# Layer 0's late modulation blocks moved from TensorE strips to running sums on VectorE, under a scheduler with three new rules

## The chip, the cores and the metric

The kernel runs on one core of a Trainium2 chip. The time of a kernel is the device time of one execution in microseconds (us), and what is given is the median of several executions. TensorE (PE in the rows) multiplies, VectorE (DVE) and ScalarE (ACT) do the elementwise work, SyncE (SP) and GpSimd (POOL) issue the transfers between HBM and the core's memory.

## The reference

A trunk of two layers over 256 context tokens and 256 latent tokens, D = 1024, float32. What matters here of each layer `i`:

```python
mod_l = jnp.split(sc @ ada_w[i] + ada_b[i], 6, axis=-1)          # sc = silu(c), one row
mod_c = jnp.split(sc_ctx @ ada_w[i] + ada_b[i], 6, axis=-1)      # the same for the context
y_l, y_c = hybrid_mixer(modulate(x, mod_l[0], mod_l[1]), modulate(ctx, mod_c[0], mod_c[1]), ...)
x = layer_norm(ALPHA * x + mod_l[2][:, None] * y_l, ln1_g[i], ln1_b[i])
x = layer_norm(ALPHA * x + mod_l[5][:, None] * swiglu(modulate(x, mod_l[3], mod_l[4]), ...), ...)
```

So the modulation is a product of two rows of length 1024 with a 1024 x 6144 matrix. Its blocks of 512 columns are numbered 0 to 11; blocks 0 to 3 are needed at the very start of a layer, blocks 4 to 11 only when the mixer's output projection ends and in the feed-forward part (FFN). The mixer has a Mamba-2 branch (convolutions, states by chunk), grouped-query attention and differential attention, merged by gates.

## The kernel before

**Work on the engines.** Every dense product is made in three fp32r passes: a weight tile is loaded raw, ScalarE copies its high part to a fp32r tile and VectorE subtracts that from the raw tile to get the low part (`load_w`, L756). So nearly each 512 KB of weights needs one ACT `CAST` and one DVE `TENSOR_TENSOR` `w<-w,w` before TensorE can use it. All other elementwise work of the branches (convolution taps in `conv`, L1149, softmax, rope, decay masks, chunk states in `chunk_state`, L1194) is on VectorE and ScalarE too.

**Order.** Nothing is issued as the code runs. Each operation is recorded in a `Plan`, with the buffers it touches; `schedule` (L312) then runs a list scheduler over modelled costs, in stretches of WINDOW modelled ns, tries TRIES = 8 sets of priorities for each stretch and keeps the best, and `emit` writes the instructions in that order. Each engine then runs its own list strictly in order on the chip and waits where an operand is not there. `pick` (L579) chooses an engine's next operation by priority, if its buffers fit (`allowed`, L503); `begin` (L649) books how long it takes and when it lands. Priorities follow the place of an operation in the recorded order, counted in TensorE time.

**Modulation.** There are two ways to make a block. `ada_parts` (L884) loads eight 128 x 512 tiles of the matrix and multiplies each on TensorE, four tiles side by side in strips of 32 columns of the array (`MATMUL ps<-s,s 128*32 128x512` in the rows, 8 records for a group of four, as an fp32 product is two). `ada_sums` (L922) loads the same tiles, and VectorE multiplies each by a column of `cond` (name `tiny`) and adds it to a running sum (`acc`, name `s`): for a sum one `TENSOR_SCALAR s<-s,tiny 128x512` and seven `SCALAR_TENSOR_TENSOR s<-s,tiny,s 128x512`; a group of four sums ends in one group of strips against `ones` (name `cst`) and four transposes. Before, layer 0 takes `ada_parts` for all twelve blocks and layer 1 takes `ada_sums`. Both use the same buffers of tag `aw`, eight at most.

**Where the late blocks stand in the recorded order.** In layer 0 the generator `ada_steps` is advanced beside the mixer, by the TensorE time that was spent:

```python
owed = advance(rest, owed + RATIO[i] * (spent() - s0))
owed2 = advance(adas, owed2 + 0.06 * (spent() - s0))
```

`advance` runs a generator until the TensorE time of what it recorded covers the cost that it was given.

Of the kernel before, what the change touches and what calls it, by code (L numbers as in the profile page):

```python
# [37 lines left out]
HOP, SLACK, SPARE = 300, 10000, 1  # L38
ENTER, LEAVE = 130, 90
GAP, REACH, BUMP = 200, 20000, 1.0  # L40
TRIES, WINDOW, AHEAD, WEIGHT = 8, 60000, 60000, 0.03

CAP = {"raw": 6, "aw": 8, "aw0": 32, "wh": 6, "wl": 6, "d": 6, "ada": 2, "row": 6, "yr": 3, "xa": 3, "re": 4}
RATIO = (1.52, 1.42)
# [373 lines left out]
class _State:  # L418
# [4 lines left out]
    def __init__(self, plan):  # L423
# [38 lines left out]
        self.cols, self.strip, self.order, self.mark, self.work = {}, False, [], 0, 0.0  # L462
        self.prio = None

    def copy(self):
        s = _State.__new__(_State)
        for k, v in self.__dict__.items():
            if k in ("plan", "room", "fifo", "prio"):
                pass
            elif k in ("load", "queue", "idle"):  # L470
                v = {c: x.copy() for c, x in v.items()}
            elif isinstance(v, (list, dict, np.ndarray)):
                v = v.copy()
            s.__dict__[k] = v
        s.mark = len(s.order)
        return s
# [23 lines left out]
                        break  # L500
        return best

    def allowed(self, b):  # L503
        c = b.cls
        if self.used[c] + b.units > self.room[c]:
            return False
        if b.cap and self.count[c, b.tag] >= b.cap:
            return False
        spot = None
        if c == "s2":  # L510
            spot = self.place(b)
            if spot is None:
                return False
        cur = self.cur
        if b.first > cur:
            seg = self.load[c][cur:b.first]
            if seg.max() + b.units > self.room[c]:
                return False
            if c == "s2":
                whole, part = b.units == 4, b.units if b.units < 4 else 0  # L520
                broken = sum(self.part_use) + (part > 0 and spot[0] == 4)
                small = self.small[cur:b.first]
                need = np.maximum((small + part + 3) // 4 + SPARE, broken)
                if ((seg - small) // 4 + whole + need).max() > self.plan.sizes["s2"]:
                    return False
        return True
# [52 lines left out]
    def pick(self, e):  # L579

        ops, sizes, q = self.plan.ops, self.plan.sizes, self.queue[e]
        skipped, pick, full = [], None, set()
        while q:
            item = heapq.heappop(q)
            new = [b for b in ops[item[1]].bufs if not self.held[b.seq] and b.cls in sizes]
            later = next((b for b in new if b.cap and self.fifo[b.cls, b.tag][self.head[b.cls, b.tag]] is not b), None)
            if later is not None:
                self.parked[later.seq] = self.parked.get(later.seq, ()) + (item[1],)
                continue
            if not new or (all(self.allowed(b) for b in new) and (len(new) < 2 or self.fits(new))):  # L590
                pick = item[1]
                break
            skipped.append(item)
            if len(skipped) > (24 if e == "SP" else 200):
                break
        for item in skipped:
            heapq.heappush(q, item)
        if pick is not None:
            for b in new:
                self.take(b)  # L600
        return pick

    def run(self, until):
        plan, ops = self.plan, self.plan.ops
        sizes, prio = plan.sizes, self.prio
        wait, running, frees, free = self.wait, self.running, self.frees, self.free
        heapq.heapify(wait)
        n = len(ops)
        while self.left and self.t < until:
            t = self.t  # L610
            while wait and wait[0][0] <= t:
                k = heapq.heappop(wait)[1]
                heapq.heappush(self.queue[ops[k].eng], (prio[k], k))
            while running and running[0][0] <= t:
                k = heapq.heappop(running)[1]
                self.done[k] = True
                self.left -= 1
                for b in ops[k].bufs:
                    self.bleft[b.seq] -= 1
                    if self.bleft[b.seq] == 0 and b.cls in sizes:  # L620
                        heapq.heappush(frees, (t + FREE, b.seq))
            while frees and frees[0][0] <= t:
                self.drop(plan.bufs[heapq.heappop(frees)[1]])
            while self.cur < n and self.done[self.cur]:
                self.cur += 1
            for e in self.ENGINES:
                if free[e] > t or not self.queue[e]:
                    continue
                pick = self.pick(e)
                if pick is not None:  # L630
                    self.begin(pick, e)
            nxt = []
            if wait:
                nxt.append(wait[0][0])
            if running:
                nxt.append(running[0][0])
            if frees:
                nxt.append(frees[0][0])
            nxt += [free[e] for e in self.ENGINES if free[e] > t and self.queue[e]]
            later = [x for x in nxt if x > t]  # L640
            if self.left and not later:
                if any(x <= t for x in nxt):
                    continue
                raise RuntimeError(f"no op can run at {t} ({self.left} left)")
            if later:
                self.t = min(later)
        return self

    def begin(self, k, e):  # L649
        ops, t = self.plan.ops, self.t  # L650
        op = ops[k]
        self.start[k] = t
        if op.nbytes:
            self.free[e] = t + op.dur
            self.dma_free = max(t + 1900, self.dma_free) + op.nbytes / 360.0
            end = self.dma_free + 950
        else:
            d = op.dur
            if e == "PE":
                c = int(t // TICK)  # L660
                cold = self.cols.get(c - 1, 0) < 3060
                if self.strip != op.strip:
                    d += ENTER if op.strip else LEAVE
                self.strip = op.strip
                self.cols[c] = self.cols.get(c, 0) + op.cols
                if cold:
                    d *= 2
                self.work += op.dur
            elif e != "SP":
                self.work += WEIGHT * op.dur  # L670
            end = t + d
            self.free[e] = end
        self.end[k] = end
        self.order.append(k)
        heapq.heappush(self.running, (end, k))
        for j in op.succs:
            e2 = ops[j].eng
            if op.nbytes:
                lat = 0
            elif e == e2:  # L680
                lat = 0 if e == "PE" else 127
            elif e == "PE":
                lat = 197
            elif e2 == "PE":
                lat = TO_PE
            else:
                lat = 145
            if end + lat > self.ready[j]:
                self.ready[j] = end + lat
            self.need[j] -= 1  # L690
            if self.need[j] == 0:
                heapq.heappush(self.wait, (self.ready[j], j))
# [20 lines left out]
def trunk(tc, x, c, cx, c_ctx, ada_w, ada_b, w_in, b_gate, conv_w, conv_b, dt_bias, a_log, ssm_d, norm_w,  # L713
# [5 lines left out]
    def t2(n=512, dt=F32, tag=None, cap=None):  # L719
        return plan.tile("s2", [128, n], dt, tag, cap)  # L720
# [4 lines left out]
    def th(n=128, tag=None, cap=None):  # L725
        return plan.tile("s2", [128, n], F32, tag, cap)
# [100 lines left out]
        V.tensor_copy(abias[i], ps[:, 0:48])  # L827

    def load_params(i):
        rows = [th(), th(), th()]  # L830
        r2 = lambda a: a.rearrange("(k p) -> k p", p=128)
        for o, n, src in ((C_BG, 24, r2(b_gate[i])), (C_CB, 24, r2(conv_b[i])),
                          (C_NW, 16, r2(norm_w[i])), (C_G1, 8, r2(ln1_g[i])), (C_B1, 8, r2(ln1_b[i]))):
# [13 lines left out]
        ps = psum()  # L847
# [220 lines left out]
    for (m, t0), xr in xraw.items():  # L1068
        xa = t2()
# [5 lines left out]
    for i in range(DEPTH):  # L1075
# [370 lines left out]

        def ada_steps():
            if i == 0:
                for ccs in ((4, 5, 6, 7), (8, 9, 10, 11)):
                    yield from ada_parts(0, ccs)  # L1450

        acc_d, t_d = dram([KT, 128, TN]), dram([KT, 128, TN])

# [74 lines left out]
        for d in range(KT):  # L1528
            w = load_w(w_ssm_out[i][D:2 * D, d * 128:(d + 1) * 128], KT, 128)
            ps = psd()  # L1530
            dense(ps[:, 0:TN], w, KT, lambda k: y[k])
            t, o = reload(t_d, d), reload(acc_d, d)
# [98 lines left out]
        for t0, r in segs:  # L1631
            for d in range(KT):
                xa = load_xa(xa_d, d, t0)
# [20 lines left out]
        for j0, j1 in ((0, 8), (8, 16), (16, 22)):  # L1654
# [26 lines left out]
            if j1 == 22 and not need_ctx:  # L1681
                xT_out = {(t, q): psum() for q in range(2) for t in range(2)}
                rows = {}
                for m, src in enumerate((ln2_g, ln2_b)):
                    for q in range(2):
                        rows[m, q] = t2()
                        G.dma_start(out=rows[m, q], in_=src[i][q * 512:q * 512 + 512].unsqueeze(0).to_broadcast([128, 512]))
            if need_ctx and j1 == 22:
                mc2 = mod_cols(i + 1, 0, (C_G2, C_B2, P))
# [110 lines left out]
```

## Time and profile before

| | us |
|---|---|
| median of 3 runs (2319.02 to 2319.55) | 2319.29 |
| profiled execution, its own time | 2322.81 |
| its span, first to last instruction | 2321.0 |
| TensorE busy in the span | 2263.6 |
| VectorE busy in the span | 1767.2 |
| ScalarE busy in the span | 1419.2 |

The profiled execution is 1.8 us longer than its span and 3.5 us above the median. The stages by the clock of the trace: start up to about 62 us, layer 0's mixer to about 1040, its FFN to about 1430, layer 1's mixer to about 2000, its FFN to the end. A busy time counts an instruction until its result is written; the next one of VectorE begins some 0.08 us before that, so the busy time of a full VectorE is its whole stretch, and work is counted best from start to start.

### The profile page before, as it was taken

The page shows a single profiled execution, that of the slowest core. Times are in us where ns is not written, and L with a number is a line of the kernel's source. Part 1 is how long each engine was busy: PE and PEld are TensorE (multiplying, and loading weights), DVE is VectorE, ACT ScalarE, POOL GpSimd, SP SyncE. Part 2 cuts the span into 40 slices and gives each one's busy share as a digit, 9 for nine tenths or more (in the row PEclk, how much of TensorE's full clock was granted, in tenths as well). Part 3 has the DMA queues.
Part 4 walks back from the last instruction along what each step waited for, and adds up shares of the span by engine and source line. Part 5 has one row for each costly group of instructions (what it writes and reads, how often), then busy time and mean ns, then how long its engine had stood idle before and what let it go on. Part 6 is the DMA issues. An engine that isn't in the chain of part 4 may idle for free.

```text
span 2321.0 us, 37955 instructions
## 1 busy us (share of the span) xinstructions
PE 2263.6 (98%) x13757; PEld 1914.9 (83%) x13757; DVE 1767.2 (76%) x3625; ACT 1419.2 (61%) x2873; POOL 138.7 (6%) x218
## 2 busy tenths in 40 slices
PE   8999999999999989999999999999999999999998
PEld 4876777777777778889888889888987779998997
DVE  3878856789988868799744338898789799868565
ACT  4767745677877564336424245787677687656553
POOL 3101101000100100000000000001010010000000
PEclk9999999999999999999999999999999999999999
DMA  9936454422533468896643324535643355786662
GB/s 322 290 90 192 147 142 142 110 78 83 157 96 91 141 177 268 282 312 179 215 121 100 99 76 130 148 112 171 182 130 100 97 137 158 202 266 192 195 183 88
DMA packets 516956, 371.48 MB, mean 160 GB/s; under 512 B 20739, under 2 KB 464515, under 8 KB 516769
## 3 DMA queue, kind: packets, MB, share of 16 engines
q1 hardware_dynamic: 503360, 329.63, 48.0%
q0 software_dynamic: 13408, 39.43, 5.9%
q8 instruction: 108, 1.77, 0.3%
q14 instruction: 80, 0.65, 0.1%
HBM read 335.17 MB, written 33.82 MB: 159 GB/s over the span
## 4 chain that ended last, share of the span: by engine, by line
PE 49%; DVE 6%; ACT 4%; DMA 4%; issue 2%; SPq 0%; ACTq 0%; POOL 0%; DVEq 0%; POOLq 0%
PE ps L415 49%; DVE s L415 3%; ACT s L415 2%; ACT shared L415 2%; DVE shared L415 2%; DMA s<-dram 1%; DMA shared<-dram 1%; DVE w L415 1%; DMA s<-in_ada_w_dram 1%; ACT w L415 1%; DVE tiny L415 0%; DMA w<-in_w_in_dram 0%; DMA w<-in_w_o_dram 0%; SPq L415 0%; POOL s L415 0%
## 5 line engine op out<-in xcount | busy, mean ns | idle before, releaser
L415 PE MATMUL ps<-s,w 128*128 128x512 f32 (+1 forms) x7560 | 1537.6, 355 | 3.2 <-DVE s L415 2.1
L415 PEld LDWEIGHTS ps<-s,w 128*128 128x128 f32 x7560 | 1238.7, 189 | 218.1 <-issue 30.0
L415 ACT CAST w<-w 128x1024 fp32r<-128x1024 f32 (+3 forms) x488 | 454.6, 940 | 399.8 <-DVE w L415 221.0
L415 DVE TENSOR_TENSOR w<-w,w 128x1024 fp32r<-128x1024 f32 (+3 forms) x488 | 528.4, 1087 | 194.6 <-PE ps L415 105.7
L415 PE MATMUL ps<-shared,w 128*128 128x256 f32 x2544 | 337.6, 285 | 5.4 <-ACT shared L415 5.3
L415 PEld LDWEIGHTS ps<-shared,w 128*128 128x128 f32 x2544 | 323.1, 193 | 8.6 <-ACT shared L415 6.6
L415 ACT ACTIVATE s<-s 128x512 f32<-128x512 f32 x424 | 260.3, 629 | 40.7 <-DVE s L415 30.5
L415 PE MATMUL ps<-s,s 128*64 128x128 f32 (+6 forms) x1888 | 243.1, 344 | 15.2 <-DVE s L415 11.9
L415 DVE TENSOR_TENSOR s<-s,s 128x512 f32<-128x512 f32 (+2 forms) x300 | 199.5, 680 | 38.1 <-ACT s L415 35.0
L415 PEld LDWEIGHTS ps<-s,s 128*64 128x64 f32 (+3 forms) x1888 | 151.9, 153 | 78.2 <-issue 23.7
L415 DVE SCALAR_TENSOR_TENSOR s<-ps,misc,s 128x510 f32<-128x510 f32 (+2 forms) x188 | 139.0, 741 | 5.5 <-ACT s L415 4.3
L415 DVE TENSOR_TENSOR s<-s,ps 128x512 f32<-128x512 f32 x116 | 78.7, 682 | 76.3 <-ACT s L415 48.4
L415 PE MATMUL ps<-w,s 128*128 128x512 f32 (+1 forms) x576 | 129.2, 374 | 2.5 <-DVE w L415 2.1
L415 DVE TENSOR_TENSOR shared<-shared,shared 128x256 f32<-128x256 f32 (+1 forms) x249 | 100.6, 416 | 30.6 <-ACT shared L415 28.2
L415 PEld LDWEIGHTS ps<-w,s 128*128 128x128 f32 x576 | 101.0, 191 | 21.8 <-DVE w L415 3.3
L415 DVE SCALAR_TENSOR_TENSOR s<-s,tiny,s 128x512 f32<-128x512 f32 x146 | 106.6, 746 | 8.8 <-DMA s<-in_ada_w_dram 7.2
L415 ACT ACTIVATE shared<-shared 128x256 f32<-128x256 f32 (+1 forms) x225 | 91.2, 415 | 25.1 <-DVE shared L415 21.9
L415 DVE TENSOR_TENSOR s<-ps,s 128x256 fp32r<-128x256 f32 (+1 forms) x200 | 83.7, 438 | 29.1 <-ACT s L415 22.7
L415 ACT ACTIVATE s<-ps,tiny 128x512 f32<-128x512 f32 x114 | 77.9, 689 | 40.3 <-DVE tiny L415 30.5
L415 POOL DMA_DIRECT2D s<-dram x96 | 71.9, 752 | 480.9 <-PE ps L415 232.2
L415 ACT CAST s<-ps 128x256 fp32r<-128x256 f32 (+1 forms) x200 | 72.6, 394 | 37.4 <-PE ps L415 29.3
L415 DVE SCALAR_TENSOR_TENSOR shared<-ps,misc,shared 128x256 f32<-128x256 f32 (+2 forms) x144 | 66.7, 478 | 27.9 <-PE ps L415 21.0
(111 smaller groups left out, 1647.2 us busy)
## 6 DMA issues: line engine op xcount, KB each, us to landing
w<-in_w_in_dram SPq DMA_DIRECT2D x196, 512.0 KB, 4.2
s<-in_ada_w_dram SPq DMA_DIRECT2D x192, 256.0 KB, 5.5
w<-in_ffn_w_in_dram SPq DMA_DIRECT2D x88, 512.0 KB, 4.0
s<-dram POOLq DMA_DIRECT2D x96, 256.0 KB, 5.4
s<-dram SPq DMA_DIRECT2D x64, 256.0 KB, 5.4
w<-in_w_ssm_out_dram SPq DMA_DIRECT2D x32, 512.0 KB, 5.4
w<-in_ffn_w_out_dram SPq DMA_DIRECT2D x32, 512.0 KB, 4.1
shared<-dram SPq DMA_DIRECT2D x112, 128.0 KB, 3.9
```

Of the source, the lines that this page charges most:

```text
L415: getattr(attr[op.eng], fn)(*[real(v) for v in args], **{a: real(v) for a, v in kw.items()})
```

## The change

In layer 0, blocks 4 to 11 go through `ada_sums`, two blocks and two rows (latent, context) to a group of four sums. The scheduler's model changes: a DMA's landing is 1250 ns (SP) or 2450 ns (POOL) after its bytes, where both were 950; each of the two queues may have eight transfers open, and the next issue waits for the oldest (`lanes`); VectorE and ScalarE do not touch the same PSUM bank in turn within 145 ns (`bank`); an operation that takes several new buffers counts them together (`more`). WINDOW falls from 60000 to 40000. Layer 1's parameter rows and the last norm's rows share buffers of the tags `xa` and `re`.

```diff
-TRIES, WINDOW, AHEAD, WEIGHT = 8, 60000, 60000, 0.03
+TRIES, WINDOW, AHEAD, WEIGHT = 8, 40000, 60000, 0.03
+LAND = {"SP": 1250, "Pool": 2450}
...
+            busy = 0.0
+            if e == "DVE" or e == "Act":
+                for b in ops[item[1]].bufs:
+                    if b.cls == "ps":
+                        other, end = self.bank.get(b.seq, (e, 0.0))
+                        if other != e and end > self.t:
+                            busy = max(busy, end)
+            if busy:
+                heapq.heappush(self.wait, (busy, item[1]))
+                continue
...
-                if free[e] > t or not self.queue[e]:
+                if free[e] > t or not self.queue[e] or e in self.lanes and self.lanes[e][0] > t:
...
-            end = self.dma_free + 950
+            end = self.dma_free + LAND[e]
+            self.lanes[e] = self.lanes[e][1:] + (max(end, self.lanes[e][-1]),)
...
+            if e == "DVE" or e == "Act":
+                for b in op.bufs:
+                    if b.cls == "ps":
+                        self.bank[b.seq] = (e, end + 145)
...
-        rows = [th(), th(), th()]
+        rows = [th(tag="xa", cap=CAP["xa"]) if i else th() for _ in range(3)]
...
-                for ccs in ((4, 5, 6, 7), (8, 9, 10, 11)):
-                    yield from ada_parts(0, ccs)
+                yield from ada_sums(0, [((cc, cc + 1), 2) for cc in (4, 6, 8, 10)])
...
-                        rows[m, q] = t2()
+                        rows[m, q] = t2(tag="re", cap=CAP["re"])
```

**What moves on VectorE.** The place is layer 0's first group of convolutions and the attention beside it. Names: `ps_..._misc` rows are taps of a convolution, `tiny_6_121` is `cond`, rows with it are running sums, other `tiny` rows belong to a softmax, `shared` and `s2` are tiles of up to 256 and of 512 columns. Before, at the second convolution's taps:

```order
SCALAR_TENSOR_TENSOR s2_215_992<-ps_214_838,misc_121_303,s2_215_992 128x2x254
TENSOR_TENSOR shared64_2_1003<-shared64_2_1003,cst_0_295 128x256
TENSOR_TENSOR s2_197_1022<-s2_198_952,s2_196_1014 128x256
SCALAR_TENSOR_TENSOR s2_215_992<-ps_214_838,misc_121_303,s2_215_992 128x2x255
TENSOR_TENSOR shared64_2_1003<-s2_198_952,cst_0_295 128x256
TENSOR_REDUCE tiny_224_1040<-ps_225_1024 128x1
TENSOR_REDUCE tiny_220_1044<-ps_221_1027 128x1
TENSOR_SCALAR tiny_224_1040<-tiny_224_1040 128x1
SCALAR_TENSOR_TENSOR s2_215_992<-ps_214_838,misc_121_303,s2_215_992 128x2x255
```

Now, at the taps of a convolution of the same group:

```order
SCALAR_TENSOR_TENSOR s2_357_1649<-ps_356_999,misc_121_257,s2_357_1649 128x2x254
TENSOR_SCALAR s2_319_1636<-s2_319_1636,tiny_320_1608 128x512
SCALAR_TENSOR_TENSOR s2_333_1506<-s2_338_1613,tiny_6_121,s2_333_1506 128x512
SCALAR_TENSOR_TENSOR s2_334_1514<-s2_338_1613,tiny_6_121,s2_334_1514 128x512
SCALAR_TENSOR_TENSOR s2_357_1649<-ps_356_999,misc_121_257,s2_357_1649 128x2x255
TENSOR_TENSOR s2_318_1678<-ps_322_1665,s2_316_1673 128x2x128
TENSOR_TENSOR s2_317_1680<-ps_322_1665,s2_315_1671 128x2x128
SCALAR_TENSOR_TENSOR s2_291_1405<-s2_294_1351,tiny_6_121,s2_291_1405 128x512
TENSOR_TENSOR s2_318_1678<-ps_326_1638,s2_316_1673 128x2x128
SCALAR_TENSOR_TENSOR s2_291_1405<-s2_295_1361,tiny_6_121,s2_291_1405 128x512
SCALAR_TENSOR_TENSOR s2_333_1506<-s2_339_1660,tiny_6_121,s2_333_1506 128x512
SCALAR_TENSOR_TENSOR s2_291_1405<-s2_329_1373,tiny_6_121,s2_291_1405 128x512
```

Running sums now stand between the taps. Counted over VectorE's whole list: from the first tap to the first product of a chunk state (`TENSOR_TENSOR` `s<-s,shared` 128x512) there were 197 instructions, and now there are 302: 179 of the old kinds, 106 `SCALAR_TENSOR_TENSOR` and 14 `TENSOR_SCALAR` of the running sums, and three small additions of `ada_b`. Six more of the sums' instructions stand ahead of the first tap and two far behind.

**What moves on TensorE.** The place is the strips of the same blocks. Before, sixteen groups of four stood among the dense products (`w4` tiles are weights), one of them:

```order
MATMUL ps_331_1571<-s2_38_372,w4_330_1150 128x512
MATMUL ps_202_805<-s2_358_1172,s2_7_81 32x512
MATMUL ps_202_805<-s2_359_1177,s2_7_81 32x512
MATMUL ps_202_805<-s2_360_1187,s2_7_81 32x512
MATMUL ps_202_805<-s2_361_1197,s2_7_81 32x512
MATMUL ps_331_1571<-s2_40_532,w4_330_1150 128x512
```

Now four groups stand there, each at the end of four sums, one of them:

```order
MATMUL ps_385_1069<-s2_47_547,w4_383_894 128x512
MATMUL ps_222_1154<-s2_202_651,cst_0_428 32x512
MATMUL ps_222_1154<-s2_203_646,cst_0_428 32x512
MATMUL ps_222_1154<-s2_212_827,cst_0_428 32x512
MATMUL ps_222_1154<-s2_213_783,cst_0_428 32x512
MATMUL ps_224_1168<-id_1_89,s2_223_1165 128x128 x4
MATMUL ps_245_1179<-s2_186_1071,s2_196_984 128x256
```

Twelve groups of strips have left TensorE's list and eight transposes have come.

## Rows read from the trace of the kernel before

**Rows 1.** The page's head and part 1: span; busy us (share) x instructions by engine.

```profile
span 2321.0 us, 37955 instructions
PE 2263.6 (98%) x13757; PEld 1914.9 (83%) x13757; DVE 1767.2 (76%) x3625; ACT 1419.2 (61%) x2873; POOL 138.7 (6%) x218
```

**Rows 2.** Stretches A:B; length, busy us (x instructions) by engine, clock, DMA share, GB/s.

```profile
0.00:62.19 62.19, 53.67 (x278) 32.78 (x279) 27.19 (x92) 29.00 (x58) 18.38 (x38) 1.00 1.00 325
62.19:156.39 94.20, 93.50 (x641) 77.24 (x640) 79.36 (x198) 69.68 (x160) 10.82 (x16) 1.00 0.68 204
156.39:300.00 143.61, 140.20 (x801) 105.48 (x799) 117.77 (x285) 103.72 (x239) 16.90 (x26) 1.00 0.54 162
300.00:850.00 550.00, 537.82 (x2860) 422.74 (x2859) 436.20 (x1005) 371.75 (x829) 45.19 (x67) 1.00 0.41 114
850.00:1000.00 150.00, 149.00 (x669) 121.75 (x668) 123.33 (x174) 69.20 (x99) 2.20 (x4) 1.00 0.87 282
1000.00:1400.00 400.00, 398.34 (x2051) 338.69 (x2050) 238.83 (x373) 159.24 (x229) 0.00 (x0) 1.00 0.49 150
1400.00:2000.00 600.00, 586.88 (x3964) 514.79 (x3964) 527.70 (x1161) 446.06 (x983) 39.97 (x61) 0.99 0.50 139
2000.00:2300.00 300.00, 294.74 (x2432) 292.51 (x2431) 206.29 (x325) 168.37 (x274) 2.19 (x4) 0.99 0.68 198
...
1500.00:1600.00 100.00, 98.90 (x691) 86.41 (x692) 96.12 (x242) 88.29 (x217) 7.93 (x12) 0.98 0.41 119
```

**Rows 3.** Timeline of VectorE, layer 0's first taps and first chunk state: start, length.

```profile
62.19 0.74 DVE L415 SCALAR_TENSOR_TENSOR s<-ps,misc,s 128x508 f32<-128x508 f32 x1
62.85 0.41 DVE L415 SCALAR_TENSOR_TENSOR shared<-shared,shared 128x256 f32<-128x256 f32 x1
...
156.39 1.29 DVE L415 TENSOR_TENSOR s<-s,shared 128x512 f32<-128x512 f32 x2 [1.45 <-ACT s L415]
```

**Rows 4.** Who VectorE waited for, 62.19 to 156.39: total us, times, longest.

```profile
DVE w L415 <- PE ps L415: 5.4, 2, 2.8
DVE s L415 <- ACT s L415: 3.2, 7, 0.8
```

**Rows 5.** Layer 1's running sums, by form over the span: busy us, mean ns, idle before.

```profile
L415 DVE SCALAR_TENSOR_TENSOR s<-s,tiny,s 128x512 f32<-128x512 f32 x146 | 106.6, 746 | 8.8 <-DMA s<-in_ada_w_dram 7.2
L415 DVE TENSOR_SCALAR s<-s,tiny 128x512 f32<-128x512 f32 x80 | 38.5, 485 | 1.5 <-DMA s<-in_ada_w_dram 1.0
```

**Rows 6.** Timeline of VectorE in layer 1's running sums: one accumulator five times running.

```profile
920.29 0.48 DVE L415 TENSOR_SCALAR s<-s,tiny 128x512 f32<-128x512 f32 x1
920.81 3.90 DVE L415 SCALAR_TENSOR_TENSOR s<-s,tiny,s 128x512 f32<-128x512 f32 x5
```

**Rows 7.** TensorE's strips and transposes by form, 156.39 to 400; two timeline rows.

```profile
L415 PE MATMUL ps<-s,s 128*32 128x512 f32 x72 | 9.6, 605 | 0.0
L415 PE MATMUL ps<-id,s 128*128 128x128 f32 x64 | 9.2, 274 | 0.6 <-ACT shared L415 0.5
...
66.52 1.92 PE L415 MATMUL ps<-s,s 128*32 128x512 f32 x16
...
85.03 1.06 PE L415 MATMUL ps<-s,s 128*32 128x512 f32 x8
```

**Rows 8.** Stretches around a fall of the clock, columns as in Rows 2.

```profile
815.00:822.60 7.60, 6.00 (x44) 4.47 (x42) 5.21 (x15) 4.40 (x10) 0.73 (x1) 1.00 0.64 174
822.60:832.60 10.00, 6.38 (x30) 4.95 (x32) 3.97 (x9) 6.14 (x12) 0.75 (x2) 1.00 0.36 89
832.60:836.10 3.50, 3.50 (x27) 2.98 (x24) 0.61 (x2) 2.74 (x5) 1.49 (x2) 0.51 0.16 9
```

More of the change, by code (lines that the diff above doesn't have):

```diff
@@ L463, in __init__ @@
         self.prio = None
+        self.lanes = {e: (0.0,) * 8 for e in ("SP", "Pool")}
+        self.bank = {}
     def copy(self):
@@ L501, in place, with allowed @@
         return best
-    def allowed(self, b):
+    def allowed(self, b, more=0):
         c = b.cls
@@ L516, in allowed @@
             seg = self.load[c][cur:b.first]
-            if seg.max() + b.units > self.room[c]:
+            if seg.max() + b.units + more > self.room[c]:
                 return False
@@ L589, in pick @@
                 continue
-            if not new or (all(self.allowed(b) for b in new) and (len(new) < 2 or self.fits(new))):
+            busy = 0.0
[8 more added lines that the diff above has]
+                continue
+            more = [sum(o.units for o in new if o.cls == b.cls) - b.units for b in new] if len(new) > 1 else (0,)
+            if not new or (all(self.allowed(b, x) for b, x in zip(new, more)) and (len(new) < 2 or self.fits(new))):
                 pick = item[1]
@@ L639, in run @@
             nxt += [free[e] for e in self.ENGINES if free[e] > t and self.queue[e]]
+            nxt += [v[0] for e, v in self.lanes.items() if v[0] > t and self.queue[e]]
             later = [x for x in nxt if x > t]
```

## The prediction, made before the changed kernel ran

> **What bounds the kernel now.** I read the page's first part, then busy times by stretch, then VectorE's timeline and waits in the stretch that the change fills. TensorE is busy 98% of the span and VectorE 76% [rows 1]. The mean hides the stages. In layer 0's FFN (1000 to 1400) TensorE is busy 398 of 400 us and VectorE 239: TensorE alone sets the pace there. In the mixers VectorE is nearly as full as TensorE: 96.12 us of 100 at 1500, 123.33 of 150 at 850 [rows 2]. Layer 1's running sums ran from about 850 on [rows 6] and into the FFN, where VectorE has room. Layer 0's new ones go elsewhere: between its first convolution tap, at 62.19, and its first chunk state, at 156.39 [rows 3]. There VectorE was busy 79.36 of 94.20 us [rows 2], so it had 14.8 us to spare; its waits were short ones for a result of TensorE or ScalarE [rows 4].
>
> **The running sums.** Eight blocks times two rows make 16 sums, each of one `TENSOR_SCALAR` and seven `SCALAR_TENSOR_TENSOR`: 16 and 112 instructions. By the new list 14 and 106 of them stand between the two places named. A `SCALAR_TENSOR_TENSOR` has a mean of 746 ns, a `TENSOR_SCALAR` 485 [rows 5]. That is until its result is written; the next instruction starts earlier. The first tap starts at 62.19, lasts 0.74, and the next instruction starts at 62.85, 0.66 later [rows 3]. So I take 0.66 and 0.40 from start to start. Where one accumulator is used five times running, five take 3.90 us, (3.90 - 0.75) / 4 = 0.79 each [rows 6]; in the new list the accumulators mostly alternate with each other or with other work, so 0.66 is nearer. 106 x 0.66 + 14 x 0.40 = 76 us.
>
> The old kinds between the two places fall from 197 instructions to 179, 72 us in proportion to the 79.36. So VectorE has 148 us of work where it had a stretch of 94.2. It runs its list in order, and the weight halves, taps and softmax rows that TensorE waits for stand between and behind the sums; TensorE has the same dense products there. So VectorE's list sets the length of this stretch. At the best share that a row shows, 96 of 100 [rows 2], it takes 148 / 0.96 = 154 us, **60 us more**. Bounds: VectorE never idle, 148, +54; its old spare 14.8 kept besides, 163, +69; and with 0.79 for each accumulation 14 more, +83. I take +60, since independent sums fill most of the gaps, while waits for their tiles remain (8.8 us before 146 in layer 1 [rows 5]).
>
> The chip's price can be weighed against a rule here. The Trainium skill (VectorE: DVE Perf Modes, "Mode 1× (REGULAR) — the baseline") says that an operation on two fp32 tensors yields one element per lane and clock of 0.96 GHz, which makes 0.53 us of 512 elements, an estimate from that page. By it the accumulations would take 14 us less and the stretch would grow by about 45. The trace shows 0.66 for such an instruction, which holds the fixed part of each instruction too, so the row decides.
>
> **The strips.** Sixteen groups of four strips leave TensorE in the mixer and four come, with eight transposes. Two groups together last 1.92 us and one 1.06, so a further group costs 0.86 [rows 7]. Of the sixteen, nine (72 records) stood behind 156.39 [rows 7], where TensorE is the fuller engine: 9 x 0.86 = 7.7 us go, the last group's four transposes come at 9.2 / 64 = 0.14 us each [rows 7], **-7**. The other seven stood in the stretch that VectorE now sets, and save nothing there. The evacuations, 2 more `ps` tiles copied on ScalarE (69.68 busy of 94.20 [rows 2]), lie beside VectorE's list.
>
> **The scheduler.** Landing times, queue turns and PSUM turns change the order everywhere, at no instruction's cost. What a better order can give back is TensorE's idle time in the middle of the program: behind 156.39 it is 3.4 + 12.2 + 1.0 + 1.7 + 13.1 + 5.3 = 36.7 us, without the start and the last 21 us [rows 2]. A part of it is VectorE's and ScalarE's full load, which no order removes. I take a third, **-12**; the bounds are -37 and, since other choices among the eight tries can also fall worse, +10. The shared buffers of the parameter rows delay small loads that nothing waits for soon: nothing, and up to 2 us if a norm waits for its rows.
>
> **The sum.** The profiled span of 2321 + 60 - 7 - 12 = 2362; with 1.8 around it 2364, and 3.5 less for the median: **2360 us**. With the bounds, +54 - 7 - 37 = +10 and +83 - 7 + 0 = +76, this case alone reaches from 2329 to 2395, most of it 2340 to 2380.
>
> **Rivals.** *TensorE does not need VectorE so soon.* If VectorE's old work in the stretch has slack towards TensorE, the sums run late without holding a product, and the strips' TensorE time is what counts. Then sixteen groups go and four come, 12 x 0.86 = 10.3, eight transposes cost 1.1 [rows 7], and the order gives 12: 2319.3 - 21 = 2298. For it: TensorE was busy 93.50 of 94.20 us there, so it had a backlog [rows 2]. Against it: the surplus is 148 - 94 = 54 us, more than half of TensorE's work in the stretch, while at most six prepared weight tiles wait in buffers (`CAP`, `wl`). It decides where the first chunk state starts: near 157 this rival holds, near 216 mine.
>
> *The clock falls.* A TensorE that gets its operands at VectorE's pace idles often. The rows show one such case: busy 6.38 of 10 us at 822.6, then 3.5 us at a granted clock of 0.51, that is 1.2 GHz [rows 8]. If the whole stretch ran at 1.2 GHz, its products would take twice 93.5 - 6 (without seven groups of strips), 175 us, more than VectorE's 154: 21 more, 2381. Against it: at the start TensorE had 278 records in 62 us where the next stretch had 641 in 94, and kept 1.00 [rows 2]. A few falls would hide behind VectorE. The Trainium skill (TensorE: Matmul & The Clock Gate, "HAM oscillation — how this bites in real kernels") says that a TensorE left waiting is taken back to half its clock; the rows of the fall agree, the start's thin load does not show it.
>
> *The loads queue up.* 64 loads of the modulation matrix now stand in SP's list within the stretch, in long runs between weight tiles; each needs one of eight buffers that VectorE frees at 2 x 0.66 = 1.3 us a tile. A weight tile behind fifteen of them comes up to 20 us late, and its halves after that: 20 more, 2380. For it: SP issues in order. Against it: the new order books queue turns.
>
> **How the numbers follow.** My case 65%, no need of VectorE 10%, the clock 8%, the loads 17%. Differences under 0.2% (4.6 us) cannot be told from no change. The rival that is faster carries the 10% for faster; of my own case hardly anything lies within 4.6 us of the time before, 3%; the rest, 87%, is slower. The range goes from the foot of my case, 2326, over both slower rivals and most of its upper bound, 2392; what is left out is the faster rival and a tail above.
>
> **What would show it.** Right: VectorE busy 95% or more from the first tap to the first chunk state, that stretch some 154 us long (148 to 169) and TensorE with gaps in it that end at VectorE's `w` or `s` tiles; 9 strip groups fewer behind it; layer 0's FFN and layer 1 as long as before or a little shorter. Wrong: a stretch below 120 us, or later stages that give back more than 37 us. The clock's rival would show as 0.5 over much of the stretch, the loads' as VectorE waiting for ScalarE's casts and these for weight tiles.

## The result, and the profile after

| | before | after |
|---|---|---|
| median on the same chip, us | 2319.42 | 2347.38 (2342.5 to 2352.75, 4 runs) |
| ratio | | 1.0118, 95% interval 1.0098 to 1.0139 |
| profiled execution / its span | 2322.81 / 2321.0 | 2349.04 / 2347.2 |
| first tap to first chunk state | 94.20 | 149.00 |
| from there to the end | 2164.6 | 2139.5 |

The change makes the kernel 28 us slower; forecast were 41 us, 2360, with 2326 to 2392 as the range. The page's head and part 1 of the changed kernel answer to [rows 1]:

```profile
span 2347.2 us, 37789 instructions
PE 2258.2 (96%) x13669; PEld 1922.0 (82%) x13669; DVE 1841.1 (78%) x3753; ACT 1416.7 (60%) x2875; POOL 138.6 (6%) x218
```

TensorE lost 88 matmuls and 5 us of busy time, VectorE gained 128 instructions and 74 us, and the span is 26 us longer. Nothing of that says where. The two marks in VectorE's timeline, as in [rows 3], do (start, length):

```profile
58.66 0.74 DVE L416 SCALAR_TENSOR_TENSOR s<-ps,misc,s 128x508 f32<-128x508 f32 x1
...
207.66 0.67 DVE L416 TENSOR_TENSOR s<-s,shared 128x512 f32<-128x512 f32 x1
```

The first tap comes 3.5 us earlier than before, the first chunk state 51.3 us later. The stretches of the changed kernel, with the columns of [rows 2]:

```profile
58.66:207.66 149.00, 111.62 (x621) 88.49 (x620) 146.56 (x304) 77.23 (x169) 9.82 (x15) 0.81 0.61 180
207.66:300.00 92.34, 88.55 (x540) 66.78 (x538) 89.28 (x246) 71.01 (x178) 10.82 (x16) 1.00 0.33 94
300.00:850.00 550.00, 547.31 (x2874) 435.71 (x2874) 455.86 (x1032) 378.93 (x849) 47.57 (x72) 1.00 0.42 118
850.00:1000.00 150.00, 147.86 (x725) 120.15 (x724) 124.78 (x188) 78.65 (x125) 9.28 (x15) 1.00 0.86 271
...
1400.00:2000.00 600.00, 592.88 (x3933) 520.35 (x3932) 524.44 (x1141) 444.72 (x971) 38.65 (x59) 1.00 0.49 139
```

In the first row VectorE is busy 146.56 of 149.00 us and TensorE only 111.62: VectorE sets the pace of this stretch, in which before TensorE was busy 93.50 of 94.20 [rows 2]. In the other rows TensorE is at 96 to 99.5% again, and in two of them fuller than before (547.31 against 537.82 of 550, 592.88 against 586.88 of 600). What VectorE does in the stretch, by form (busy us, mean ns, idle before), beside [rows 5]:

```profile
L416 DVE SCALAR_TENSOR_TENSOR s<-s,tiny,s 128x512 f32<-128x512 f32 x106 | 76.1, 745 | 0.6 <-DMA s<-in_ada_w_dram 0.6
L416 DVE TENSOR_SCALAR s<-s,tiny 128x512 f32<-128x512 f32 x20 | 9.4, 475 | 0.0
```

All 106 accumulations are here (14 of the 20 `TENSOR_SCALAR` belong to sums too). Who waits for whom in the stretch (total us, times, longest), first VectorE's waits, then TensorE's:

```profile
DVE misc L416 <- PE ps L416: 1.1, 1, 1.1
DVE s L416 <- DMA s<-in_ada_w_dram: 0.6, 1, 0.6
DVE s L416 <- ACT s L416: 0.5, 1, 0.5
DVE shared L416 <- ACT shared L416: 0.2, 1, 0.2
```

```profile
PE ps L416 <- DVE s L416: 25.8, 9, 7.6
PE ps L416 <- ACT s L416: 5.1, 4, 3.0
PE ps L416 <- ACT shared L416: 4.9, 3, 3.1
PE ps L416 <- DVE shared L416: 1.2, 2, 1.0
```

VectorE waits for almost nothing, 2.4 us, where before it waited 12.9 us in this stretch ([rows 4] show the two longest of seven lines); TensorE waits 37.0 us, 27.0 of them for VectorE's results directly. So the waiting has changed sides. It ends at `s` and `shared` tiles, not at the weight halves `w`, which the prediction had named as well. What the `s` tiles are, the strips on TensorE tell, from the start to 207.66, by form (busy us, mean ns, idle before):

```profile
L416 PE MATMUL ps<-s,cst 128*32 128x512 f32 x24 | 4.9, 908 | 14.5 <-DVE s L416 14.5
```

`cst` is `ones`: these are three of the four closing groups of the sums. TensorE, which runs its list in order, stood 14.5 us in front of them for the sums themselves; the other `s` waits are for VectorE's remaining work, queued among the sums. Behind 207.66 one of layer 0's closing groups, 8 records, is left where 72 strips stood [rows 7] (by form, from there to 1000):

```profile
L416 PE MATMUL ps<-s,cst 128*32 128x512 f32 x8 | 1.1, 604 | 0.0
```

### The profile page after: what moved, and what is told of

The parts are those of the page before. It is cut to its first block, busy times and chain, and to the rows that moved or that the text cites. A ratio compares the mean times of both kernels' runs of the same rounds, so it can differ in the third digit from the quotient of the medians.

```text
span 2347.2 us, 37789 instructions
## 1 busy us (share of the span) xinstructions
PE 2258.2 (96%) x13669; PEld 1922.0 (82%) x13669; DVE 1841.1 (78%) x3753; ACT 1416.7 (60%) x2875; POOL 138.6 (6%) x218
## 4 chain that ended last, share of the span: by engine, by line
PE 79%; DVE 8%; DMA 5%; issue 4%; ACT 4%; SPq 1%; POOL 0%; ACTq 0%; DVEq 0%; POOLq 0%
PE ps L416 79%; DVE s L416 4%; ACT s L416 2%; DVE shared L416 2%; DMA s<-dram 1%; ACT shared L416 1%; DVE w L416 1%; DMA w<-in_w_o_dram 1%; DMA shared<-dram 1%; ACT w L416 1%; DMA s<-in_ada_w_dram 1%; DVE tiny L416 1%; SPq L416 1%; DMA shared<-in_ln_b_dram 0%; POOL shared L416 0%
## 5 line engine op out<-in xcount | busy, mean ns | idle before, releaser
L416 PE MATMUL ps<-shared,w 128*128 128x256 f32 x2544 | 330.4, 285 | 4.9 <-ACT shared L416 4.9
L416 PE MATMUL ps<-s,s 128*64 128x128 f32 (+5 forms) x1760 | 225.2, 325 | 12.1 <-DVE s L416 6.8
L416 DVE SCALAR_TENSOR_TENSOR s<-s,tiny,s 128x512 f32<-128x512 f32 x258 | 188.6, 750 | 10.4 <-DMA s<-in_ada_w_dram 8.8
L416 DVE SCALAR_TENSOR_TENSOR s<-ps,misc,s 128x508 f32<-128x508 f32 (+2 forms) x188 | 139.5, 743 | 4.5 <-ACT s L416 2.8
```

The source lines that it names most:

```text
L416: getattr(attr[op.eng], fn)(*[real(v) for v in args], **{a: real(v) for a, v in kw.items()})
```

## The experiments

All times are medians, with the ratio to the kernel before on the same chip and its 95% interval.

**Taking the sums out again.** `e1_strips_new_rules`: the new scheduler with the old strips. "New rules" stands from here on for everything in the change but the sums: the changes of the scheduler's model, WINDOW and the shared buffers. No run takes these apart.

```diff
-                yield from ada_sums(0, [((cc, cc + 1), 2) for cc in (4, 6, 8, 10)])
+                for ccs in ((4, 5, 6, 7), (8, 9, 10, 11)):
+                    yield from ada_parts(0, ccs)
```

> The changed kernel with layer 0's late blocks back on TensorE strips, under the new scheduler rules. Theory A (the running sums make VectorE set the first convolution stretch, the new rules give a little back): the stretch from the first tap to the first chunk state falls back from 149 to about 94 us, the 7 us of strips come back, and the rules keep their 18: about 2300 us (2292 to 2312), faster than before. Theory B (the new rules cost the time, the sums are hidden): it stays at about 2345.

Measured 2298.56 us (0.9918, 0.9902 to 0.9935). The stretch, columns as above:

```profile
59.52:149.14 89.62, 89.42 (x612) 74.88 (x611) 81.53 (x192) 72.97 (x168) 11.34 (x17) 1.00 0.74 210
```

Without the sums TensorE is busy 89.42 of 89.62 us and the clock stays at 1.00. The sums are the loss, not the new rules: with the same rules they cost 49 us (42 with another seed, below).

**The sums alone.** `e2_sums_old_rules`: the kernel before with `ada_sums` for blocks 4 to 11, the diff above the other way round.

> The kernel before with the running sums alone, old scheduler rules. Theory A: the stretch grows by about 55 and the strips behind it save 7: about 2367 us (2355 to 2380), slower than the changed kernel. Theory B: about 2310, as only ten us of strips go and the sums are hidden.

Measured 2349.07 us (1.013, 1.0115 to 1.0145), 18 less than expected and 6 under the range. The stretch:

```profile
65.34:215.47 150.13, 111.00 (x634) 86.60 (x633) 148.48 (x308) 74.96 (x165) 10.57 (x16) 0.83 0.56 168
```

VectorE is 99% busy and the stretch as long as in the changed kernel, so the rules have no part in it. The miss lies behind the first chunk state: 2130.0 us to the end where the old rules otherwise take 2163 to 2169 (table below). That is the one kernel of the old rules that does so, and why stays open.

**Half of VectorE's work, all of the loads.** `e4_half_the_sums` leaves out seven of the eight products of each context row's sum in layer 0, 56 accumulations, so the late modulation of the context is not computed; all 64 loads stay.

```diff
-                        else:
+                        elif r == 0 or i:
                             V.scalar_tensor_tensor(acc[r], w, col, acc[r], ALU.mult, ALU.add)
```

> The changed kernel with the context rows' sums cut to their first tile of eight: 56 of the 112 accumulations are left out (the context's late modulation is therefore not computed), while all 64 tiles are loaded in the same order of code. Theory A: 56 x 0.66 = 37 us of VectorE's work leave the stretch, 149 becomes about 112: about 2310 us (2303 to 2325). Theory C (the 64 loads ahead of the weight tiles in SP's queue cost the time): unchanged, about 2345.

Measured 2313.56 us (0.9979, 0.9969 to 0.999). The stretch:

```profile
57.85:177.72 119.87, 101.85 (x631) 82.30 (x629) 109.49 (x238) 71.47 (x157) 10.21 (x15) 0.94 0.75 228
```

The stretch is 29.1 us shorter. It holds 54 accumulations, 52 fewer than in the changed kernel (four of the 56 left out had stood outside it); their busy time fell from 76.1 to 39.2 us (by form, columns as before):

```profile
L416 DVE SCALAR_TENSOR_TENSOR s<-s,tiny,s 128x512 f32<-128x512 f32 x54 | 39.2, 742 | 0.0
```

So most of the work that left, 29 of 37 us, came off the stretch, and the theory that the loads alone make the stretch long, which would have left the time near that of the change, falls. VectorE has 10 us of waits again, and 7.02 of them are one wait, which hangs on a load. ScalarE, then VectorE:

```profile
93.29 0.62 ACT L416 CAST w<-w 128x512 fp32r<-128x512 f32 x1 [7.05 <-DMA w<-in_w_in_dram]
...
94.40 0.16 DVE L416 RECIPROCAL tiny<-tiny 128x1 f32<-128x1 f32 x1 [7.02 <-ACT shared L416]
```

ScalarE stood 7.05 us in front of a cast for a weight tile, and VectorE for what ScalarE does behind that cast. Once VectorE has less to do, a late weight tile does hold the stretch; whether the loads of the modulation matrix made it late was not tested. This run also lets VectorE free the matrix tiles sooner, so it is no clean test of the queue by itself. The changed kernel's own waits are: there ScalarE waits for weight tiles

```profile
ACT w L416 <- DMA w<-in_w_in_dram: 2.2, 2, 1.5
```

2.2 us in all, and VectorE 0.6 us for tiles of the matrix (above).

**The same sums, spread.** `e3_sums_spread` keeps all 128 instructions and the new rules, and only moves where the sums are recorded. `advance` lets a generator run until the TensorE time of what it recorded covers the cost; a sum has next to none until its closing strips, so one call lets a whole group of four sums through (read from the code). The edit takes a single step of the generator (four tiles of the matrix) per 45 us of TensorE time:

```diff
-            owed2 = advance(adas, owed2 + 0.06 * (spent() - s0))
+            owed2 += spent() - s0
+            while owed2 > 45000:
+                owed2 -= 45000
+                next(adas, None)
```

> The changed kernel with the same 128 instructions of running sums recorded at a steady pace over layer 0's mixer (half a block for each 45 us of TensorE time) and not in its first 100 us. Theory A: VectorE has some 10 to 20% to spare in most of the mixer, so most of the 55 us goes: about 2315 us (2302 to 2330). Theory B: the place makes no difference, about 2347.

Measured 2292.41 us (0.9883, 0.9869 to 0.9898): 55 us under the changed kernel, 27 under the one before, and better than the range expected. Its stretch, and the middle of the mixer, where most of the sums now are:

```profile
61.64:149.39 87.75, 86.64 (x589) 77.39 (x588) 85.62 (x209) 70.21 (x166) 11.57 (x17) 1.00 0.48 138
...
300.00:850.00 550.00, 542.79 (x2894) 424.85 (x2893) 496.21 (x1111) 383.14 (x852) 47.22 (x71) 1.00 0.48 140
```

In the first of them the sums have left 13 accumulations (by form, columns as before):

```profile
L416 DVE SCALAR_TENSOR_TENSOR s<-s,tiny,s 128x512 f32<-128x512 f32 x13 | 9.4, 738 | 0.0
```

In the middle VectorE takes 60 us more than before (496.21 against 436.20 [rows 2]) and TensorE is at 98.7% all the same: this stretch had 114 us of room on VectorE where the early stretch had 15.

**The spread under the old rules.** `e5_spread_old_rules` is `e2_sums_old_rules` with the edit of `e3_sums_spread`.

> The kernel before with the late blocks as running sums, recorded a quarter group at a time (one yield of ada_sums per 45 us of TensorE time) as in e3_sums_spread, but under the old scheduler's rules. If the place of the sums is what counts and the new rules give a mean of 12 us, the time is that of e3_sums_spread plus 12: about 2304 us (2296 to 2314), below the kernel before, and the first chunk state starts between 148 and 158 us. If the spread pays only under the new rules (they know the banks and the queue turns that the sums' loads and results need), the time is at or above that of before, 2319 to 2330.

Measured 2328.44 us (1.0036, 1.002 to 1.0053), as the second of the two expectations had it; the start of the first chunk state, 153.40, is as the first had it. The stretch is healed here too:

```profile
63.08:153.40 90.32, 86.04 (x574) 75.44 (x573) 82.05 (x187) 65.64 (x146) 9.07 (x14) 1.00 0.50 140
```

But the rest, from the first chunk state to the end, takes 2169.2 us against 2142.0 under the new rules: TensorE is busy 10.6 us more there (2113.9 against 2103.3) and idle 16.6 us more (55.3 against 38.7). Spreading the sums undoes the early loss under either set; a gain over strips came only with the new rules. That is one order under the old rules, and the reason that the expectation gives (banks and queue turns) was not tested.

**How much an order is worth by chance.** The scheduler draws its eight sets of priorities from random numbers with seed 7. Other seeds give other orders of the same program. Each of these has the edit

```diff
-        rng = np.random.default_rng(7)
+        rng = np.random.default_rng(11)
```

(or 23): on the kernel before, on `e1_strips_new_rules`, on the changed kernel and on `e3_sums_spread`.

> The kernel before with another seed for the scheduler's random priorities; same instructions, another order. If the 20 us by which the new rules beat the old ones on the same work (the strips on TensorE) are the rules' own, another seed moves this one by a few us: 2312 to 2326. If they are luck of the draw, the seeds scatter by ten to twenty: 2295 to 2330.

> As the run before, a third seed under the old rules. Rules: 2312 to 2326. Draw: anywhere from 2295 to 2330.

> The strips under the new rules (2298.6 with the first seed) with another seed. Rules: 2293 to 2306, below every seed of the old rules. Draw: scatter that overlaps the old rules' seeds, some run at 2310 or above.

> As the run before, a third seed under the new rules. Rules: 2293 to 2306. Draw: overlap with the old rules' seeds.

> The changed kernel with the second seed. If the starved stretch is a matter of where the sums stand in the recorded order and not of the draw, the stretch is again about 149 us (145 to 156) and this run lies 40 to 55 us above the strips with the same seed (2314.7): 2350 to 2368. If the draw made it, the stretch is below 130.

> The sums spread over the mixer with the second seed. If sums at a steady pace are worth the strips' 10 us of TensorE time, this is 5 to 10 below the strips with the same seed (2314.7): 2302 to 2312. If the 6 us that they gained with the first seed were luck, it is 2315 or more.

In the table "rest" is the profiled span less the start of the first chunk state, and "TensorE" its busy time in the whole profiled span.

| kernel | median us | ratio to before, interval | rest, us | TensorE, us |
|---|---|---|---|---|
| strips, old rules, seed 7 (before) | 2319.42 | 1 | 2164.6 | 2263.6 |
| seed 11, `s1_old_rules_seed11` | 2319.25 | 1.001 (1.0 to 1.0019) | 2163.4 | 2263.2 |
| seed 23, `s2_old_rules_seed23` | 2324.3 | 1.0037 (1.0024 to 1.005) | 2165.6 | 2263.3 |
| strips, new rules, seed 7, `e1_strips_new_rules` | 2298.56 | 0.9918 (0.9902 to 0.9935) | 2146.3 | 2250.0 |
| seed 11, `s3_new_rules_seed11` | 2314.66 | 0.9993 (0.9983 to 1.0003) | 2149.9 | 2254.5 |
| seed 23, `s4_new_rules_seed23` | 2309.38 | 0.9971 (0.996 to 0.9981) | 2156.0 | 2253.8 |
| early sums, new rules, seed 7 (the change) | 2347.38 | 1.0118 (1.0098 to 1.0139) | 2139.5 | 2258.2 |
| seed 11, `s5_change_seed11` | 2356.93 | 1.0175 (1.0156 to 1.0193) | 2145.1 | 2258.6 |
| spread sums, new rules, seed 7, `e3_sums_spread` | 2292.41 | 0.9883 (0.9869 to 0.9898) | 2142.0 | 2242.4 |
| seed 11, `s6_spread_seed11` | 2293.45 | 0.99 (0.9884 to 0.9917) | 2140.5 | 2239.9 |
| early sums, old rules, `e2_sums_old_rules` | 2349.07 | 1.013 (1.0115 to 1.0145) | 2130.0 | 2255.8 |
| spread sums, old rules, `e5_spread_old_rules` | 2328.44 | 1.0036 (1.002 to 1.0053) | 2169.2 | 2253.6 |

The runs are from several chips, on which the kernel before itself had medians from 2316.66 to 2320.03, so the ratios compare better than the times. With strips, the three seeds lie 0.37% (9 us) apart under the old rules and 0.75% (17 us) under the new. So the 21 us between the kernel before and `e1_strips_new_rules` overstate the new rules: on the mean of three seeds they give 2320.99 - 2307.53 = 13 us, and 13 by the ratios too. With a scatter that wide, three seeds do not fix that mean well: the slowest under the new rules (0.9993) is not told apart from the fastest under the old (1). TensorE's busy time tells the two sets apart more clearly: 2250.0 to 2254.5 us under the new rules, 2263.2 to 2263.6 under the old, for the same 13757 matmuls. By their medians both orders of the changed kernel are slower than all six kernels with strips, and both spread orders under the new rules are faster than all six. The stretch of `s5_change_seed11` is starved once more, longer than the 145 to 156 us expected:

```profile
56.87:216.53 159.66, 114.06 (x648) 91.97 (x647) 151.88 (x309) 76.76 (x168) 10.57 (x16) 0.81 0.60 179
```

Its time is as expected, 42 us above the strips of its seed. Of the other seeds, `s1_old_rules_seed11` and `s2_old_rules_seed23` fit both theories, `s3_new_rules_seed11` is where chance would put it, `s4_new_rules_seed23` lies between the two, and `s6_spread_seed11` came out 9 us below the range expected.

**A loss near the end.** In the 60 us around layer 1's first norm TensorE is idle for 6 to 12 us in the kernels with the new rules and for 4 to 7 in those with the old. TensorE's timeline of the changed kernel there (start, length, in brackets the idle time before and its releaser):

```profile
2131.04 4.17 PE L416 MATMUL ps<-shared,cst 128*128 128x256 f32 x8 [6.03 <-DVE shared L416]
2140.12 10.06 PE L416 MATMUL ps<-shared,w 128*128 128x256 f32 x57 [4.91 <-ACT shared L416]
```

Eleven us are idle at two waits. The theory was that the parameter rows of layer 1, which now share the three buffers of the tag `xa`, hold up the norm's loads; `s7_spread_xa5` gives `e3_sums_spread` five of them (`"xa": 3` to `"xa": 5` in `CAP`).

> The sums spread, first seed (2292.4), with five residual buffers of tag xa instead of three. In layer 1's first norm the new rules' kernels lose 12 to 17 us of TensorE time where the old ones lose 6 to 8, and the last residual tiles are issued late there. If the three buffers hold these loads back, that stage loses 5 to 8 less: 2284 to 2289. If not, the time moves only by the draw, 2285 to 2300, with the loss in that stage unchanged.

Measured 2291.16 us (0.9888, 0.9874 to 0.9903), not told apart from `e3_sums_spread`, and TensorE is idle in the norm for as long, 9.3 and 8.7 us. `e3_sums_spread`, then `s7_spread_xa5`, columns as in [rows 2]:

```profile
2044.48:2104.48 60.00, 50.74 (x372) 48.28 (x371) 46.34 (x94) 32.36 (x58) 0.00 (x0) 0.86 0.64 180
...
2043.00:2103.00 60.00, 51.27 (x374) 48.08 (x373) 45.83 (x91) 29.13 (x53) 0.00 (x0) 0.89 0.67 189
```

The theory falls; what holds up the norm is open. The 12 to 17 and 6 to 8 us in the expectation are more than this idle time, and no row shows what else they hold.

## Why the prediction was right, and where it was off

**The bound of the early stretch: right.** VectorE 98% busy, TensorE's gaps at its results, the first chunk state at 207.66 where 216 was named for this case and 157 for the first rival. `e1_strips_new_rules` and `e3_sums_spread` show the two halves of the reason apart: the sums must be there, and they must be recorded there. `e2_sums_old_rules` shows that the long stretch needs nothing else of the change.

**Its size: 5 us too large.** The work was right: 148 us forecast, and 146.56 busy. The term that was mis-sized is the share: 96 of 100 was taken from the best row of before, while VectorE reached 146.56 of 149.00. Its own waits nearly vanish (2.4 us against 12.9), as one would expect where sums that wait for a load at most stand in the gaps. So +54.8 instead of +60, close to the lower bound of the working, VectorE never idle, +54. `s5_change_seed11` has 159.66 with 151.88 busy, 95%, so the share differs from order to order, and the 96% taken lies between the two.

**The price of an accumulation: right.** In VectorE's timeline of the changed kernel five in a row read (the view does not tell the sums apart; `ada_sums` records the two rows of a tile one after the other, on two sums)

```profile
91.46 3.40 DVE L416 SCALAR_TENSOR_TENSOR s<-s,tiny,s 128x512 f32<-128x512 f32 x5
```

(3.40 - 0.74) / 4 = 0.665 us from start to start, where 0.66 was taken; 0.79, the upper bound, was measured on one sum used running [rows 6]. The Trainium skill's 0.53 us, an estimate from its page VectorE: DVE Perf Modes ("Mode 1× (REGULAR) — the baseline"), would have made the growth about 45; the row decides against using it as an instruction's whole price.

**Strips: right. Order: 5 us too small, and not of the kind named.** The rest fell by 25.1 us where -7 for the strips and -12 for the order were forecast. (With the first tap 3.5 us earlier, which the sum had not, +54.8 - 25.1 - 3.5 is the span's +26.2.) The rest of the kernel before, of the changed kernel and of `e2_sums_old_rules`, columns as in [rows 2]:

```profile
156.39:2321.00 2164.61, 2116.44 (x12843) 1804.88 (x12840) 1660.65 (x3336) 1320.50 (x2656) 109.53 (x164) 0.99 0.52 153
...
207.66:2347.20 2139.54, 2097.87 (x12778) 1800.19 (x12776) 1667.17 (x3362) 1311.35 (x2651) 118.46 (x180) 0.99 0.52 152
...
215.47:2345.50 2130.03, 2093.70 (x12757) 1797.22 (x12756) 1660.63 (x3352) 1309.52 (x2652) 109.04 (x164) 1.00 0.53 152
```

TensorE's busy time in it fell by 18.6 us and its idle time by 6.5 (48.2 to 41.7). Some 8 of the 18.6 are the strips, as forecast: 72 records took 9.6 us [rows 7], the 8 that are left take 1.1, and four transposes come. So about 17 us are left for the order, and of these only 6.5 are idle time, where the prediction looked for all 12. It let the order act on idle time alone, "at no instruction's cost"; but with the strips kept, the new rules' orders have TensorE busy 9 to 14 us less in the whole span (table). Why the same matmuls take less busy time in these orders is open. The 12, a third of the idle time, was a guess; that it came near 17 is in part luck, and no single pair could have verified it, since the seeds differ by more. By the means of the rest, 13.8 us come with the new rules (2164.5 to 2150.7, strips in both) and 9 more with the sums (to 2141.8, the four kernels with all the sums, the new rules and three `xa` buffers). `e2_sums_old_rules` stands against a clean account: under the old rules its rest is shorter than the changed kernel's, in busy and in idle time, and why is open.

The upper end of the working, 2395, left out the order's own bound of +10; nothing turns on it.

**The rivals.** That TensorE does not need VectorE so soon is refuted by the waits and the landmark. The loads' queue is refuted by the waits of the changed kernel (ScalarE 2.2 us for weight tiles, VectorE 0.6 for the matrix); `e4_half_the_sums` adds that the time goes with VectorE's work, and that a late weight tile can cost 7 us once VectorE has room. The clock did fall, as its rival had it, but hidden. Windows of the changed kernel, columns as above, the granted clock third from the end:

```profile
70.00:91.60 21.60, 18.64 (x137) 16.14 (x135) 20.51 (x42) 10.68 (x23) 6.54 (x9) 1.00 0.84 245
91.60:112.05 20.45, 9.73 (x36) 6.32 (x37) 19.36 (x40) 10.01 (x26) 0.00 (x0) 0.50 0.66 191
112.05:146.20 34.15, 29.31 (x209) 25.58 (x207) 33.93 (x73) 18.72 (x43) 1.66 (x3) 1.00 0.56 174
146.20:156.40 10.20, 7.77 (x22) 5.69 (x23) 10.20 (x19) 3.77 (x10) 0.54 (x1) 0.50 0.36 107
163.30:173.50 10.20, 6.34 (x22) 3.66 (x23) 10.20 (x23) 2.99 (x7) 0.00 (x0) 0.50 0.59 176
190.60:207.60 17.00, 10.29 (x28) 6.56 (x29) 17.00 (x42) 8.72 (x20) 0.54 (x1) 0.50 0.34 103
```

TensorE ran at 1.2 GHz for 57.9 of the 149 us, in four rows; ahead of the first it was busy 18.64 of 21.60 us at 2.4 GHz. In the four rows VectorE is busy 56.76 us; the other 1.09 are one wait for a result of TensorE, in the first row. So within these rows the slow clock held VectorE back by 1.1 us at most, and a TensorE at 2.4 GHz would have waited for the same results; that is read from the rows, and no kernel was run that holds the clock up. The Trainium skill (TensorE: Matmul & The Clock Gate, "HAM oscillation — how this bites in real kernels") says that a TensorE kept waiting is taken back to half its clock; these rows agree.

**What the prediction did not see.** It called VectorE nearly as full as TensorE in the mixers. In layer 0's mixer its own rows say otherwise: VectorE is busy 436.20 of 550 us and 123.33 of 150, 79 and 82%, beside TensorE's 98 and 99 [rows 2]; only layer 1's mixer is tighter, 527.70 of 600. That is the room which `e3_sums_spread` uses. The early stretch had a like share free, 14.8 of 94.20 us; it is short, and all of the sums came into it. And it asked what the sums cost where they stand, and not why they stand there. `advance` pays its generator in TensorE time, and the new work has next to none; that is visible in the code, and the edit of `e3_sums_spread` follows from it.

## What to carry to other kernels

When work moves from the engine that is full on the mean to one that has room on the mean, look at the stretch in which it lands: 74 us of VectorE work made the early stretch 55 us longer where VectorE had 15 to spare; spread over the mixer, which had 114 to spare in its middle alone, the same work left the kernel 55 us faster than that. A planner that paces side work by the cost on one engine lets work of another engine through all at once; hand such work out in small fixed steps (here four tiles of the matrix per 45 us of TensorE time). Compare two schedules over several seeds before a gain of under 1% is put down to a rule.

## What the runs showed of the hardware

The granted clock fell to 0.50 four times within 149 us, for 57.9 us together, and in these rows VectorE, which set the pace, lost at most 1.1 us to it. VectorE was busy for 95 to 99% of 149 to 160 us where independent sums stood between dependent work (146.56 of 149.00, 148.48 of 150.13, 151.88 of 159.66 us). The seed of the order alone moved the time of one and the same program by up to 0.75%, some 17 us, and TensorE's busy time for the same matmuls by up to 4.5 us under the new rules. One order can scatter more than another: nine executions of `e5_spread_old_rules` lie between 2319.45 and 2334.74 us, 24 of the kernel before on one chip between 2312.87 and 2319.54.
